# Part sums for the down product, emitted ahead of the S1 T1 product in each gate and up step

## The chip, the cores and the metric

The kernel runs on one core of a Trainium2 chip. The metric is the device time of one execution in microseconds; the times given are medians of several runs. The profile is one execution taken by the hardware profiler, with each engine's instructions, what they waited for, and the TensorE clock that was granted.

## The reference

An encoder trunk of two layers on a sequence of 1024 tokens of width 1024, in float32. Layer 0 has a chunked gMLP mixer, layer 1 a chunked attention with a relative bias; behind each stands a SwiGLU FFN, and the change lies in that FFN alone:

```python
def _swiglu_ffn(x, g_norm, w_gate_up, w_down):
    h = _rms_norm(x, g_norm)
    gate, up = jnp.split(h @ w_gate_up, 2, axis=-1)
    return (jax.nn.silu(gate) * up) @ w_down
```

The hidden width is 2816, 22 tiles of 128.

## The kernel before

Every matmul works on float32 numbers split into a high and a low part, so that a product of two 128 x 128 blocks takes three matmuls (high by high, high by low, low by high). The high part is made by a cast on ScalarE, the low part by a subtraction on VectorE (`split`, L116 to L118).

The gate and up product is done with a seven-product scheme for 2 x 2 blocks. One step `f` makes one tile of gate and one of up, for all 1024 tokens, with 7 products of 12 matmuls each: A11 B11, S2 T2, S1 T1, A12 B21, S3 T3, S4 B22 and A22 T4, in this order on TensorE. The A's and S's come from the step's two weight tiles (`quad_load`): A11 and A12 are the gate tile, S1 to S4 sums of gate and up made on GpSimd (L517, L518, L524, L525), A22 half of the up tile. The B's and T's come from the input, are made once, and stay in SBUF. There is one place for each kind of split weights, so the split of the next step's S12, A, S34 and A22 (`quad_s12`, `quad_a`, `quad_s34`, `quad_a22`) can begin when this step's products with them are through. The two raw tiles have one place each too: the next step's weights are loaded when this step's low parts are made.

The products of a step go into three PSUM banks, `pa`, `pb` and `pc`. `pb` takes S2 T2, S3 T3 and A22 T4 in turn: L793 and L804 read the sum out between them (`bu`), L833 reads the last (`yy`). `pc` takes S1 T1, is copied by ScalarE at L795 (`ac`), and then takes S4 B22, read at L823. `pa` takes A11 B11 (copied at L791) and A12 B21, which the gate reads (L701, and the SiLU at L702). `up` (L707, L708) makes y, the input of the down product.

For 16 of the 22 tiles of y the down product uses the same scheme, and needs sums and split parts of y. They are made during the gate and up loop by `y_parts`: when the odd step of a pair of tiles is done, five parts for that pair go into the list `todo`, and the steps that follow take them out with `some()`. They are `t12` (L683, L684: the sums for T1 and T2 in the tile `ty`), `t34` (L688, L691, a cast on ScalarE at L692, L693, and one transfer to DRAM at L694), and three times `out` (a cast at L676, the low part at L678, and two transfers, L679 and L680), for the second tile of the pair (`yo`), the first (`ye`) and `ty`. The first pair's parts are taken from f = 4 on, the last pair's at f = 18 and 19, in each of the two layers, 16 pairs in all.

In the kernel before, `some()` is called three times a step: behind the split of S12 (L797), behind the split of A (L802), and behind the split of S34 (L831). The step after a pair has even f and takes `t12`, `t34` and `out(1)`; the next has odd f and takes `out(0)` and `out(2)`.

The program's text isn't the order in which an engine works. A planner takes the instructions in the order in which they are emitted, works out what each waits for, and lays out one queue for each engine; on the chip each engine goes through its queue in order and waits for other engines by semaphores. SyncE's queue (SP) issues all transfers of this loop.

Of the kernel before, what the change touches and what calls it, by code (L numbers as in the profile page):

```python
# [49 lines left out]
class Trunk:  # L50
# [570 lines left out]
    def ffn(self, x, layer, sqp):  # L621
        nc, a = self.nc, self.a
        with ExitStack() as st:
# [16 lines left out]
            def bank():  # L640
                return psum.tile([P, 512], F32, name="ps")
# [19 lines left out]
            def outs(f):  # L661

                places = (0, 1, 4 if f == 1 else 6, (3, 5, 7)[f % 3])
                return [xplace(j, f"{n}{f}") for j, n in zip(places, ("ac", "bu", "gg", "yy"))]
# [3 lines left out]
            def y_parts(f):  # L668

                p = (f - 2) // 2  # L670
                ye, yo = ys.pop(f), ys.pop(f + 1)
                t = self.scratch(f"ty{f}")

                def out(n, y, place):
                    hi = xplace(place, f"yh{f}_{n}", F32R)
                    nc.scalar.copy(hi, y)  # L676
                    lo = y.bitcast(F32R)
                    TT(lo, y, hi.bitcast(F32), sub)  # L678
                    nc.sync.dma_start(td[p, 2 * n], hi.bitcast(F32))  # L679
                    nc.sync.dma_start(td[p, 2 * n + 1], y)  # L680

                def t12():
                    TT(t[:, t1], ye[:, t2], ye[:, t1], sub)  # L683
                    TT(t[:, t2], yo[:, t2], t[:, t1], sub)  # L684
                yield t12

                def t34():
                    TT(ye[:, t2], yo[:, t2], ye[:, t2], sub)  # L688
                    t4 = xplace(4, f"yt{f}", F32R)
                    r = t4[:, t2].bitcast(F32)  # L690
                    TT(r, yo[:, t1], t[:, t2], sub)  # L691
                    nc.scalar.copy(t4[:, t1], r)  # L692
                    TT(t4[:, t2], r, t4[:, t1].bitcast(F32), sub)  # L693
                    nc.sync.dma_start(td[p, 6], t4.bitcast(F32))  # L694
                yield t34
                yield lambda: out(1, yo, 2)
                yield lambda: out(0, ye, 4)
                yield lambda: out(2, t, 2)

            def gate(o, s, src):  # L700
                TT(o[2][:, HALF[s]], src, rbc[:, HALF[s]], mul)  # L701
                nc.scalar.activation(o[2][:, HALF[s]], o[2][:, HALF[s]], AF.Silu)  # L702

            def up(o, s, other, eng=None):

                y = o[3][:, HALF[s]]
                TT(y, y, rbc[:, HALF[s]], mul)  # L707
                TT(y, y, o[2][:, HALF[s]], mul)  # L708
# [28 lines left out]
            def prod(ps, A, b, start=False, stop=True):  # L737
                self.product(ps, q[A], (b, B), range(4), start, stop, True)
# [35 lines left out]
            def some(n=1):  # L774
                for _ in range(n):
                    if todo:
                        todo.pop(0)()

            for f in range(2, FT):
                more = f + 1 < FT  # L780
                if more:
                    qn = self.quad_load(layer, f + 1)
                    self.quad_places(qn, self.QUAD)
                else:
                    self.wlist, self.wnext = wl + (self.att_w if layer == 0 else []), 0
                o = outs(f)
                ac, bu, gg, yy = o
                pa, pb, pc = bank(), bank(), bank()

                prod(pa, "A11", "B11", True)  # L790
                nc.scalar.copy(ac[:, t1], pa)  # L791
                prod(pb, "S2", "T2", True)
                TT(bu[:, t1], pb, ac[:, t1], add)  # L793
                prod(pc, "S1", "T1", True)
                nc.scalar.copy(ac[:, t2], pc)  # L795
                self.quad_s12(qn) if more else self.prep_w()
                some()  # L797
                prod(pa, "A12", "B21")
                if f > 2:
                    gate(o, 0, pa)  # L800
                self.quad_a(qn) if more else self.prep_w()
                some()  # L802
                prod(pb, "S3", "T3")
                TT(bu[:, t2], pb, ac[:, t1], add)  # L804
                if f == 2:

                    bc = [bank(), bank()]
                    self.stats(None, bc[0], acc, rstd)
                    rbc = self.const.tile([P, S], F32, name="rbc")
                prod(pc, "S4", "B22", stop=True)  # L810
                if f == 2:
                    for s in range(2):
                        self.broadcast(self.hx, bc[s], rstd[:, 4 * s:4 * s + 4], rbc[:, HALF[s]], ("scr", 3))
                    for k in range(2):
                        _, _, g, y = late[k]
                        TT(g, g, rbc, mul)
                        nc.scalar.activation(g, g, AF.Silu)
                        TT(y, y, rbc, mul)
                        TT(y, y, g, mul)
                        nc.sync.dma_start(yd[k], y)  # L820
                    gate(o, 0, pa)
                TT(yy[:, t2], bu[:, t2], ac[:, t2], add)
                TT(gg[:, t2], pc, bu[:, t1], add)  # L823
                gate(o, 1, gg[:, t2])
                up(o, 1, None)
                if more:
                    self.quad_s34(qn)
                else:
                    d0 = self.down_load(layer, 0)
                    self.down_t1(d0)  # L830
                some()  # L831
                prod(pb, "A22", "T4", stop=True)
                TT(yy[:, t1], pb, ac[:, t1], add)  # L833
                up(o, 0, None)
                self.quad_a22(qn) if more else self.down_t2(d0)
                if f < FT - 4:
                    ys[f] = yy
                    if f % 2:
                        todo += y_parts(f - 1)
                else:  # L840
                    nc.sync.dma_start(yd[f], yy)
                q = qn
# [63 lines left out]
            for k in range(nq + 1):  # L906
# [22 lines left out]
                if k < nq:  # L929
# [7 lines left out]
                    else:  # L937
                        f = FT - 4 + k % 4
# [386 lines left out]
```

## Time and profile before

| | us |
|---|---|
| median of three runs | 2555.15 |
| lowest and highest run | 2554.9, 2555.91 |
| the profiled execution | 2560.03 |
| its span, first to last instruction | 2558.2 |

The mean granted TensorE clock of the profiled execution was 0.986 of full speed. In rows of instructions the columns are the start from the beginning of the span, the duration, engine, line, operation, the tile written and the tiles read, shape, and a count; in square brackets the idle time of the engine just before, and what ended it. PE is TensorE, DVE VectorE, ACT ScalarE, POOL GpSimd. Tile names drop their numbers: `wlo<-s,whi` is the low part of summed weights (S12 or S34), `wlo<-wraw,whi` that of loaded ones (A with 1024 columns, A22 with 512), `ty` the tile of T1 and T2, `yt` the tile of T4. Of the products' inputs `b1h`, `b1l`, `b2h` and `b2l` are the B's and T3, `bth` and `btl` T1 and T2, `bt` T4.

### The profile page before, as it was taken

The page shows a single profiled execution, that of the slowest core. Times are in us where ns is not written, and L with a number is a line of the kernel's source. Part 1 is how long each engine was busy: PE and PEld are TensorE (multiplying, and loading weights), DVE is VectorE, ACT ScalarE, POOL GpSimd, SP SyncE. Part 2 cuts the span into 40 slices and gives each one's busy share as a digit, 9 for nine tenths or more (in the row PEclk, how much of TensorE's full clock was granted, in tenths as well). Part 3 has the DMA queues.
Part 4 walks back from the last instruction along what each step waited for, and adds up shares of the span by engine and source line. Part 5 has one row for each costly group of instructions (what it writes and reads, how often), then busy time and mean ns, then how long its engine had stood idle before and what let it go on. Part 6 is the DMA issues. An engine that isn't in the chain of part 4 may idle for free.

```text
span 2558.2 us, 30686 instructions
## 1 busy us (share of the span) xinstructions
PE 2453.9 (96%) x11454; PEld 2018.4 (79%) x11454; DVE 1836.8 (72%) x2809; ACT 970.0 (38%) x1509; POOL 500.8 (20%) x413
## 2 busy tenths in 40 slices
PE   8999999999999999999999999989999999999997
PEld 7888888887777777788778887878877777777887
DVE  6227676688887876677777777778877778767775
ACT  5123232345433333212345555554453333332223
POOL 3001111121222222232211000000112222323411
PEclk9999999999999999999999999999999999999998
DMA  5232222232343434973312222252323434349731
GB/s 198 83 108 82 70 66 62 70 123 79 131 153 121 163 121 157 341 280 126 130 55 68 60 66 60 65 153 75 132 98 118 163 122 157 117 161 345 294 105 67
DMA packets 122390, 329.20 MB, mean 129 GB/s; under 512 B 11776, under 2 KB 44544, under 8 KB 122240
## 3 DMA queue, kind: packets, MB, share of 16 engines
q1 hardware_dynamic: 119936, 323.04, 37.1%
q10 hardware_dynamic: 2304, 4.20, 0.5%
q8 instruction: 90, 1.47, 0.2%
q14 instruction: 60, 0.49, 0.1%
HBM read 224.43 MB, written 94.37 MB: 125 GB/s over the span
## 4 chain that ended last, share of the span: by engine, by line
PE 65%; DVE 17%; DMA 6%; issue 5%; POOL 4%; ACT 3%; SPq 0%; DVEq 0%; POOLq 0%; ACTq 0%
PE ps L618 14%; PE ps L896 10%; PE pj L215 8%; PE ps L229 7%; PE ps L215 7%; DVE wlo L118 4%; DMA wraw<-wup 3%; PE pj L229 2%; PE po L1168 2%; PE ps L333 2%; PE ps L335 2%; PE ps L334 2%; PE pt L1141 2%; PE ps L456 1%; PE s L1118 1%
## 5 line engine op out<-in xcount | busy, mean ns | idle before, releaser
L117 ACT CAST whi<-wraw 128x1024 fp32r<-128x1024 f32 (+1 forms) x213 | 203.7, 961 | 365.2 <-PE ps L229 111.0
L118 DVE TENSOR_TENSOR wlo<-wraw,whi 128x1024 fp32r<-128x1024 f32 (+1 forms) x213 | 239.8, 1130 | 62.7 <-ACT whi L117 62.1
L896 PE MATMUL ps<-t,whi 128*128 128x512 f32 x896 | 278.1, 391 | 6.1 <-ACT whi L117 4.9
L517 POOL TENSOR_TENSOR s<-wraw 128x512 f32<-128x512 f32 x42 | 58.4, 1389 | 862.3 <-DMA wraw<-wup 521.0
L900 DVE TENSOR_TENSOR x<-x,ps 128x512 f32<-128x512 f32 x224 | 151.6, 684 | 74.3 <-PE ps L896 74.2
L896 PEld LDWEIGHTS ps<-t,whi 128*128 128x128 f32 x896 | 168.4, 189 | 43.4 <-ACT whi L117 5.7
L117 ACT CAST whi<-s 128x1024 fp32r<-128x1024 f32 x84 | 88.0, 1050 | 273.2 <-POOL s L518 242.6
L118 DVE TENSOR_TENSOR wlo<-s,whi 128x1024 fp32r<-128x1024 f32 x84 | 111.7, 1329 | 111.1 <-ACT whi L117 108.6
L896 PE MATMUL ps<-t,wlo 128*128 128x512 f32 x448 | 174.9, 390 | 0.0
L230 DVE TENSOR_TENSOR x<-x,ps 128x512 f32<-128x512 f32 (+1 forms) x176 | 113.2, 660 | 66.2 <-PE ps L229 62.4
L618 PE MATMUL ps<-bt,whi 128*128 128x512 f32 x336 | 116.8, 431 | 41.7 <-DVE bu L804 41.0
L618 PE MATMUL ps<-b2h,whi 128*128 128x512 f32 x368 | 147.1, 400 | 10.1 <-ACT ac L791 7.6
L215 PE MATMUL pj<-hhi,whi 128*128 128x512 f32 x368 | 151.1, 411 | 0.0
L215 PE MATMUL pj<-hlo,whi 128*128 128x512 f32 x368 | 148.1, 402 | 2.7 <-DVE hlo L118 2.7
L215 PE MATMUL pj<-hhi,wlo 128*128 128x512 f32 x368 | 146.7, 399 | 0.0
L618 PE MATMUL ps<-b1h,wlo 128*128 128x512 f32 x368 | 143.7, 390 | 2.7 <-DVE wlo L118 2.7
L396 POOL TENSOR_TENSOR mt<-mt,bbc 128x256 f32<-128x256 f32 x64 | 58.7, 918 | 445.5 <-ACT mt L395 442.5
L618 PE MATMUL ps<-b2h,wlo 128*128 128x512 f32 x368 | 145.4, 395 | 0.0
L618 PE MATMUL ps<-b2l,whi 128*128 128x512 f32 x368 | 145.4, 395 | 0.0
L618 PE MATMUL ps<-b1l,whi 128*128 128x512 f32 x368 | 143.5, 390 | 1.2 <-DVE b1l L118 1.2
L618 PE MATMUL ps<-b1h,whi 128*128 128x512 f32 x368 | 144.0, 391 | 0.1
L618 PE MATMUL ps<-bth,whi 128*128 128x512 f32 x336 | 130.7, 389 | 0.0
(367 smaller groups left out, 6490.3 us busy)
## 6 DMA issues: line engine op xcount, KB each, us to landing
t<-td SPq DMA_DIRECT2D x112, 512.0 KB, 7.8
td<-yh SPq DMA_DIRECT2D x48, 512.0 KB, 2.9
wraw<-wg SPq DMA_DIRECT2D x44, 512.0 KB, 3.6
wraw<-wup SPq DMA_DIRECT2D x44, 512.0 KB, 3.6
td<-yy SPq DMA_DIRECT2D x32, 512.0 KB, 2.7
wraw<-wds SPq DMA_DIRECT2D x32, 512.0 KB, 5.3
vd<-vt SPq DMA_DIRECT2D x32, 256.0 KB, 2.5
wraw<-wu SPq DMA_DIRECT2D x16, 512.0 KB, 3.7
```

What stands on the lines that cost most here:

```text
L117: self.nc.scalar.copy(hi, src)
L118: self.nc.vector.tensor_tensor(lo, src, hi.bitcast(F32), ALU.subtract)
L215: nc.tensor.matmul(ps[s], wt[:, c], ht[:, t], start=(kt == 0 and i == 0), stop=(kt == KT - 1 and i == 2),)
L229: nc.tensor.matmul(o, wt[:, c], yt[:, t], start=(j == 0 and i == 0), stop=(j == last and i == 2))
L230: nc.vector.tensor_tensor(x[d][:, t], x[d][:, t], o, ALU.add)
L333: nc.tensor.matmul(ps[tt], hhi[:, t], whi[:, c], start=(kt == 0), stop=False)
L334: nc.tensor.matmul(ps[tt], hhi[:, t], wlo[:, c], start=False, stop=False)
L396: nc.gpsimd.tensor_tensor(t2, t2, _bc_mid(bbc[:, g * P:(g + 1) * P], 2), ALU.add)
L517: nc.gpsimd.tensor_tensor(s12[:, HALF[0]], u[:, HALF[0]], u[:, HALF[1]], ALU.add)
L618: nc.tensor.matmul(ps, w[:, c], h, start=(start and i == pairs[0] and n == 0), stop=(stop and i == pairs[-1] and n == 2), skip_group_check ...
L896: nc.tensor.matmul(q[bank_], w[:, c], h, start=(start and i == 0 and n == 0), stop=(stop and i == 1 and n == 2), skip_group_check=True)
L900: TT(o, o, q[bank_], add)
```

## The change

In each step the three calls of `some()` are replaced by one, which stands behind the first add (L793) and ahead of the S1 T1 product. It takes three parts where f is even and two where f is odd. The parts themselves and their order in the list are the same.

```diff
                 TT(bu[:, t1], pb, ac[:, t1], add)
+                some(2 + (f + 1) % 2)
                 prod(pc, "S1", "T1", True)
                 nc.scalar.copy(ac[:, t2], pc)
                 self.quad_s12(qn) if more else self.prep_w()
-                some()
                 prod(pa, "A12", "B21")
                 if f > 2:
                     gate(o, 0, pa)
                 self.quad_a(qn) if more else self.prep_w()
-                some()
                 prod(pb, "S3", "T3")
...
                     self.down_t1(d0)
-                some()
                 prod(pb, "A22", "T4", stop=True)
```

## Rows read from the trace of the kernel before

**Rows 1.** The page's busy times: share of the span and instructions of each engine.

```profile
PE 2453.9 (96%) x11454; PEld 2018.4 (79%) x11454; DVE 1836.8 (72%) x2809; ACT 970.0 (38%) x1509; POOL 500.8 (20%) x413
```

**Rows 2.** Busy times by stretch: two pairs of steps, even then odd f.

```profile
core 0: us, PE busy (x) PEld busy (x) DVE busy (x) ACT busy (x) POOL busy (x), PEclk, DMA share, GB/s
911.40:932.80 21.40, 19.42 (x85) 15.70 (x85) 19.41 (x22) 8.88 (x12) 6.32 (x4) 1.00 0.43 150
932.80:952.50 19.70, 19.48 (x86) 15.62 (x85) 12.20 (x18) 6.13 (x9) 5.08 (x4) 1.00 0.37 131
702.40:725.20 22.80, 20.94 (x85) 16.84 (x85) 20.87 (x24) 8.86 (x12) 6.32 (x4) 0.93 0.49 168
725.20:744.30 19.10, 19.10 (x86) 15.80 (x85) 11.55 (x16) 6.61 (x10) 5.08 (x4) 1.00 0.28 104
```

**Rows 3.** Instructions in order of time, TensorE, an even step: S4 B22 and A22 T4.

```profile
925.05 0.39 PE L618 MATMUL ps<-b2h,whi 128*128 128x512 f32 x1
...
927.54 0.39 PE L618 MATMUL ps<-b2h,wlo 128*128 128x512 f32 x1
929.91 0.74 PE L618 MATMUL ps<-bt,whi 128*128 128x512 f32 x2 [1.98 <-DVE bu L804]
```

**Rows 4.** TensorE's groups: busy, mean ns, idle time ahead and what ended it.

```profile
L618 PE MATMUL ps<-b2h,whi 128*128 128x512 f32 x368 | 147.1, 400 | 10.1 <-ACT ac L791 7.6 <-ACT ac L747 1.2 <-ACT ac L795 1.1
...
L618 PE MATMUL ps<-bt,whi 128*128 128x512 f32 x336 | 116.8, 431 | 41.7 <-DVE bu L804 41.0 <-DVE bu L761 0.7
```

**Rows 5.** Instructions in order of time, VectorE, the same even step as rows 3.

```profile
914.69 0.68 DVE L683 TENSOR_TENSOR ty<-yy 128x512 f32<-128x512 f32 x1
917.16 0.69 DVE L793 TENSOR_TENSOR bu<-ps,ac 128x512 f32<-128x512 f32 x1 [1.78 <-PE ps L618]
...
918.93 1.77 DVE L688 TENSOR_TENSOR yy<-yy,yy 128x512 f32<-128x512 f32 x1
920.63 1.78 DVE L691 TENSOR_TENSOR yt<-yy,ty 128x512 f32<-128x512 f32 x1
922.52 2.13 DVE L678 TENSOR_TENSOR yy<-yy,yh 128x1024 fp32r<-128x1024 f32 x1
924.57 1.22 DVE L118 TENSOR_TENSOR wlo<-s,whi 128x1024 fp32r<-128x1024 f32 x1
925.70 0.68 DVE L693 TENSOR_TENSOR yt<-yt 128x512 fp32r<-128x512 f32 x1
...
926.91 1.21 DVE L678 TENSOR_TENSOR ty<-ty,yh 128x1024 fp32r<-128x1024 f32 x1
928.04 1.21 DVE L118 TENSOR_TENSOR wlo<-wraw,whi 128x1024 fp32r<-128x1024 f32 x1
929.17 0.68 DVE L804 TENSOR_TENSOR bu<-ps,ac 128x512 f32<-128x512 f32 x1
...
931.82 1.22 DVE L678 TENSOR_TENSOR yy<-yy,yh 128x1024 fp32r<-128x1024 f32 x1
932.96 0.69 DVE L701 TENSOR_TENSOR gg<-gg,rbc 128x512 f32<-128x512 f32 x1
```

**Rows 6.** Instructions in order of time, GpSimd: first and last sum of that step.

```profile
917.16 1.30 POOL L517 TENSOR_TENSOR s<-wraw 128x512 f32<-128x512 f32 x1 [12.85 <-DMA wraw<-wup]
...
921.94 1.62 POOL L525 TENSOR_TENSOR s<-wraw,s 128x512 f32<-128x512 f32 x1
```

**Rows 7.** Instructions in order of time, VectorE, the odd step that follows.

```profile
945.87 1.33 DVE L118 TENSOR_TENSOR wlo<-s,whi 128x1024 fp32r<-128x1024 f32 x1 [6.67 <-ACT whi L117]
```

**Rows 8.** Instructions in order of time, ScalarE, the even step of rows 3.

```profile
921.89 1.05 ACT L117 CAST whi<-s 128x1024 fp32r<-128x1024 f32 x1 [5.95 <-POOL s L518]
922.85 0.57 ACT L795 COPY ac<-ps 128x512 f32<-128x512 f32 x1
923.33 0.62 ACT L692 CAST yt<-yt 128x512 fp32r<-128x512 f32 x1
...
929.99 1.06 ACT L676 CAST yh<-yy 128x1024 fp32r<-128x1024 f32 x1 [2.34 <-DMA td<-yt]
```

**Rows 9.** Instructions in order of time, VectorE, first pair's even step in layer 0.

```profile
679.81 0.68 DVE L804 TENSOR_TENSOR bu<-ps,ac 128x512 f32<-128x512 f32 x1
680.41 1.21 DVE L678 TENSOR_TENSOR ty<-ty,yh 128x1024 fp32r<-128x1024 f32 x1
```

## The prediction

> **What bounds the kernel now.** I first read the busy shares of the page: TensorE is busy 96% of the span [rows 1], so a change can only win what TensorE waits for, or lose by making it wait more. The change touches only the gate and up loop (f = 2 to 21, twice), so the next view is the busy time by stretch, cut at the step boundaries [rows 2]. A step is 84 matmuls. Inside a product they follow each other at (927.54 - 925.05) / 11 = 0.226 us [rows 3], so a step without a wait takes 84 x 0.226 = 19.0 us. The two pairs of rows 2 take 41.1 and 41.9 us where 38.0 would do: 2.4 and 3.8 us too much in the step with even f, 0.7 and 0.1 in the step with odd f. With 16 pairs (f = 4 to 19, two layers) the whole loss is some 49 to 62 us, about 2% of the time, and that is the ceiling of any gain here.
>
> Where it goes is told by the groups of TensorE's instructions with the idle time ahead of each: the largest entry of this loop is A22 T4 waiting for the add at L804, 41.0 us in all [rows 4]. In the even step of rows 3, S4 B22 issues its last matmul at 927.54, and A22 T4 starts at 929.91, because it writes the bank that L804 reads, and L804 only ran from 929.17 to 929.85 [rows 5]. The step at 702.4 loses more than its wait, and its granted clock is 0.93 while the others have 1.00 [rows 2].
>
> Why L804 is late is read from VectorE's queue in the same step [rows 5]: from the first add (L793, 917.16) on there is no idle time. Ahead of L804 stand the second sum for T2 (between L793 and L688), L688, L691, the low part of yo (L678), the low part of the S12 weights (L118), that of T4 (L693), the gate multiply, the low part of ty (L678, 926.91), and the low part of the A weights. Three of the adds took 1.77, 1.78 and 2.13 us, where the same shapes take 0.68 and 1.21 us (L693 and the ty row), while GpSimd ran its weight sums from 917.16 to 923.56 [rows 5, 6]. In the odd step VectorE has 6.67 us of idle time in one piece [rows 7]. So the even step is VectorE's, the odd one is not.
>
> **What the order of emission decides.** This is the hinge. The rows show that the queues aren't in the order of emission; as I read them, the planner gives an engine the earliest emitted of what it holds to be ready. On ScalarE the cast of S12 (921.89) runs ahead of the copy L795 (922.85), though L795 is emitted first [rows 8]. On VectorE L683 (914.69) runs ahead of the add L793 (917.16), though it is emitted after it [rows 5]. And the low parts of ty (926.91) and ye (931.82) run in the even step, though they are emitted in the odd one [rows 5]. So emission is only a priority among ready things, and the change only matters where a part was ready and stood behind something that it is now emitted ahead of.
>
> **The change, part by part.** Nothing is added or removed: the same five parts a pair, with the same instructions and transfers, three in the even step and two in the odd one, as before (the third call of an odd step found an empty list). What moves:
>
> (1) The sums t12 (L683, L684), from behind the S12 split to behind L793. L683 already runs ahead of L793, and the rest right behind it [rows 5]. 0.
>
> (2) t34 (L688, L691, the cast L692, L693, and one transfer), from behind the A split. L688 and L691 already run right behind t12, with no weight work between them. L692 started at 923.33, as soon as the S12 cast (to 922.94) and the copy L795 (to 923.42) were through, while its input had been ready since 922.41, the end of L691 [rows 5, 8]. This is the one place where it stood behind something that it now precedes: L692 and L795 should swap on ScalarE. L692 gains 0.5 us, and L795 loses the 0.62 of L692. The S12 cast itself keeps its place unless the planner thinks L691 done before it; then it would have done so before, too, since nothing else was in ScalarE's way. L693 follows the low part of S12, which was being worked on anyway until 925.79; its price is 0, and the transfer of T4 goes out when it did. L795 would end at 923.42 + 0.62 = 924.04; S4 B22, which writes the bank that L795 reads, starts at 925.05 [rows 3]. So 0, with 1.0 us to spare; if the cover were gone, at most 0.62 us a pair. Its bounds are 0 and 16 x 0.62 = 9.9 us of loss; a gain on this edge is excluded, because no VectorE instruction leaves the stretch ahead of L804. I take 0, by the row that shows the 1.0 us.
>
> (3) The part out(1) (yo: a cast, L678, two transfers), from behind the S34 split. Its L678 is already the first long one behind L691 at 922.52, and ahead of the weights' low parts [rows 5]. 0.
>
> (4) out(0) and out(2), in the odd step, now behind the odd L793. They are still emitted after everything of the even step, and they already run there, at 926.91 and 931.82. Their rank against the even step's work is unchanged. 0.
>
> Transfers: SP's queue carries the parts' seven transfers between the loads of the next weights. These loads are emitted at the head of the step, ahead of the parts in both kernels, so no part passes a load. GpSimd gets no part, and its order of sums stays. No wait is added.
>
> The sum is 0 for each of the four. Against the profiled execution that is 2560.0 us again (a span of 2558.2 and 1.8 around it); this lies 4.9 us above the median of the three runs, 2555.15, to which I apply the 0. What a measurement of this kernel can tell from no change is about 0.2%, 5 us.
>
> A rule that speaks against the change: rows 5 and 6 show part sums of 0.68 us taking 1.78 while GpSimd works. The Trainium skill (SBUF — State Buffer, Who interferes with whom) says that a VectorE instruction with two SBUF inputs and a GpSimd instruction that reads SBUF lock each other out, the later one waiting in full. By that rule, work drawn forward into GpSimd's sums is work made dearer, and this kernel's rows agree.
>
> **The rivals.**
>
> F1, faster: the swap on ScalarE or a change of the planner's clock lets the low part of ty fall behind L804. In the first pair of layer 0 it does: L804 at 679.81, ty at 680.41 [rows 9]. Worth 928.04 - 926.91 = 1.13 us a pair, 16 x 1.13 = 18 us: 2537. For it: the order there differs from rows 5 by one rank only. Against: nothing on VectorE is moved by the change. 10%.
>
> F2, faster: the parts run where they are written, out(0) and out(2) in the idle time of the odd step. L804 of the even step comes 1.13 us sooner, and with 1.1 more from ye the last weight split too, which frees the odd step of its 0.7: 1.8 us a pair, 29 us, 2526. Against: the even step's VectorE takes whatever is ready [rows 5], and the change holds nothing back. 6%.
>
> S1, slower: the copy L795 behind the cast of T4 holds S4 B22. Price 0.62 us a pair, 9.9 us, 2565. It decides where L795 ends after S4 B22's turn. For it: TensorE waited for L795 1.1 us in all already [rows 4]. Against: 1.0 us to spare in rows 3 and 8, and a late S4 B22 is swallowed by the 2 us for which A22 T4 waits anyway. 10%.
>
> S2, slower: T4's transfer goes earlier, the place that it frees lets ye's cast (929.99, which waited for that transfer [rows 8]) go earlier, and its low part gets ahead of L804: 932.96 is the next start after 931.82, so about 1.14 us a pair, 18 us, 2573. It decides if that cast ends before 929.17 instead of 931.05. L693 can gain 1.13 us at most (by passing the low part of S12), so 1.9 us is out of reach of the rows; it can happen only in the planner's own idea of the times. 6%.
>
> S3, slower: the low parts of T4 and ty are drawn under GpSimd's sums and take 1.78 and 2.13 us for 0.68 and 1.21: 2.0 us a pair, 32 us, 2587. Against: the sums end at 923.56, and T4's cast, even swapped, ends at about 923.5 [rows 6, 8]. This is what the rule of the skill named above would do here. 2%.
>
> **How the numbers follow.** The forecast, the queue of VectorE unchanged, has 66%; that is also the rival "it doesn't do what it says" turned round: the text of the kernel changes and the order that runs does not. Time 2555.2, its own range 2550 to 2560. F1 and F2 make 16% for faster, S1, S2 and S3 18% for slower. The range takes in the forecast, F1 with its 2537 and S1 with its 2565, rounded up: 2537 to 2566. It leaves out F2, S2 and S3, 14%.
>
> **What would show it.** In the changed kernel's even steps, VectorE's instructions from L793 to L804 stand in the order of rows 5, L692 starts ahead of L795 on ScalarE, TensorE's wait for L804 stays at 41 us within some 5, and pairs take 41 to 42 us. It is wrong if ty or ye are found in odd steps or on the other side of L804 (F1, F2, S2), if TensorE's wait for L795 grows by more than a few us (S1), or if L693 or ty take twice their time (S3).

## The result and the profile after

| | us |
|---|---|
| before, median | 2555.1 |
| after, median (2507.32 to 2513.78) | 2508.05 |
| ratio after to before, 95% interval | 0.982 (0.9803 to 0.9837) |
| span of the profiled execution, before and after | 2558.2, 2512.0 |

The changed kernel is 47 us faster, just under the ceiling of 49 to 62 us that the prediction worked out from [rows 2]. The forecast was no change.

All steps from f = 4 to 19, one row a layer (in the columns of [rows 2]), in the kernel before:

```profile
662.00:998.10 336.10, 315.48 (x1346) 255.60 (x1345) 262.49 (x307) 123.22 (x161) 94.57 (x64) 0.98 0.41 144
1937.10:2274.80 337.70, 316.15 (x1346) 255.46 (x1346) 260.56 (x306) 122.94 (x161) 94.41 (x64) 0.98 0.41 143
```

And in the kernel after:

```profile
662.50:976.70 314.20, 307.27 (x1346) 251.63 (x1345) 242.05 (x306) 125.99 (x162) 96.47 (x64) 1.00 0.43 153
1913.30:2228.90 315.60, 307.43 (x1346) 251.65 (x1345) 243.09 (x308) 126.10 (x162) 95.88 (x64) 1.00 0.43 154
```

These 32 steps took 673.8 us and take 629.8: 44 of the 46 us between the spans. Unbroken they would take 32 x 19.0 = 608, so they lost 66 us and lose 22. Of the 44 us, 27 are time in which TensorE no longer waits; in the other 17 it does the same matmuls in less time, which is for the most part its clock, shown below.

The busy times by stretch of the kernel after: the pair of steps that [rows 2] show first, then the second pair, and the step with f = 19 of layer 0. Of the last, the kernel before is shown too, in the block of rows behind.

```profile
898.40:918.50 20.10, 19.33 (x85) 15.69 (x84) 16.98 (x22) 9.04 (x12) 7.02 (x4) 1.00 0.63 236
918.50:937.60 19.10, 19.10 (x86) 15.81 (x85) 13.04 (x19) 6.71 (x10) 5.09 (x4) 1.00 0.18 55
702.60:722.90 20.30, 19.38 (x86) 15.70 (x85) 18.80 (x22) 9.07 (x12) 7.01 (x4) 1.00 0.63 233
722.90:741.90 19.00, 19.00 (x85) 15.76 (x84) 12.93 (x19) 6.63 (x9) 5.10 (x4) 1.00 0.17 56
957.70:976.70 19.00, 19.00 (x86) 15.73 (x84) 12.23 (x18) 6.61 (x10) 5.08 (x4) 1.00 0.41 138
```

```profile
974.30:998.00 23.70, 20.91 (x85) 16.80 (x85) 13.33 (x18) 5.90 (x8) 5.09 (x4) 0.93 0.49 177
```

The two pairs took 41.1 and 41.9 us and take 39.2 and 39.3. Their odd steps are at the 19.0 us of 84 unbroken matmuls, the even ones lose 1.1 to 1.3 us, and f = 19 lost 4.7 us before and loses nothing now. In the even step VectorE's busy time fell from 19.41 to 16.98 us and in the odd one it rose from 12.20 to 13.04. TensorE's groups of A22 T4, before (in [rows 4]) and after:

```profile
L618 PE MATMUL ps<-bt,whi 128*128 128x512 f32 x336 | 107.4, 401 | 14.4 <-DVE bu L803 13.8 <-DVE bu L761 0.6
```

The wait for the second add (L804 before, L803 now) fell from 41.0 to 13.8 us. The busy time of these matmuls fell too, from 116.8 to 107.4 us. That is the clock: in eight of the 32 steps of the kernel before, f = 19 among them in both layers, the granted clock was 0.92 to 0.94, and in the kernel after it is 1.00 over all of them. In each of the eight the slow matmuls are those of A22 T4, right behind its wait for L804. In the step at 702.4 of [rows 2], for one, a matmul behind the wait takes 0.63 us where 0.39 is usual:

```profile
720.79 1.09 PE L618 MATMUL ps<-bt,whi 128*128 128x512 f32 x2 [1.86 <-DVE bu L804]
721.68 0.63 PE L618 MATMUL ps<-bt,wlo 128*128 128x512 f32 x1
```

So a part of these steps ran at the lower of the clock's two levels, 1.2 and not 2.4 GHz, after TensorE had stood idle (1.86 us in this row). TensorE's busy time in such a step was about 20.9 us where 19.4 was usual; eight times 1.5 us is some 12 us of the gain, by these rows.

VectorE's queue around the same even step, in order of time:

```profile
900.77 0.68 DVE L684 TENSOR_TENSOR ty<-yy,ty 128x512 f32<-128x512 f32 x1
...
901.98 0.68 DVE L688 TENSOR_TENSOR yy<-yy,yy 128x512 f32<-128x512 f32 x1
902.58 0.68 DVE L691 TENSOR_TENSOR yt<-yy,ty 128x512 f32<-128x512 f32 x1
903.36 1.23 DVE L678 TENSOR_TENSOR yy<-yy,yh 128x1024 fp32r<-128x1024 f32 x1
904.51 0.68 DVE L793 TENSOR_TENSOR bu<-ps,ac 128x512 f32<-128x512 f32 x1
905.11 1.19 DVE L693 TENSOR_TENSOR yt<-yt 128x512 fp32r<-128x512 f32 x1
906.97 1.56 DVE L678 TENSOR_TENSOR ty<-ty,yh 128x1024 fp32r<-128x1024 f32 x1 [0.68 <-ACT yh L676]
910.79 1.34 DVE L118 TENSOR_TENSOR wlo<-s,whi 128x1024 fp32r<-128x1024 f32 x1 [2.27 <-ACT whi L117]
...
913.79 1.21 DVE L678 TENSOR_TENSOR yy<-yy,yh 128x1024 fp32r<-128x1024 f32 x1
914.93 0.68 DVE L803 TENSOR_TENSOR bu<-ps,ac 128x512 f32<-128x512 f32 x1
...
922.56 0.69 DVE L683 TENSOR_TENSOR ty<-yy 128x512 f32<-128x512 f32 x1
```

The first parts aren't behind the first add, where the text of the kernel has them. The second sum for T2, L688, L691 and the low part of yo stand ahead of it, among VectorE's last work on the odd step's y, and fill the 1.78 us for which VectorE was idle there [rows 5]; and the next pair's first sum (L683) is made at 922.56, when only the even tile of that pair exists, where it used to wait for the end of the odd step ([rows 5], 914.69). Ahead of the first add the sums for T2 and T4 take 0.68 us each: they are through by 903.26, and GpSimd starts its weight sums at 903.96, as its instructions show:

```profile
903.96 1.79 POOL L517 TENSOR_TENSOR s<-wraw 128x512 f32<-128x512 f32 x1 [13.57 <-DMA wraw<-wup]
...
907.41 2.27 POOL L518 TENSOR_TENSOR s<-s,wraw 128x512 f32<-128x512 f32 x1
```

### The profile page after: what moved, and what is told of

It is laid out like the page before. It is cut to its first block, busy times and chain, and to the rows that moved or that the text cites. A ratio compares the mean times of both kernels' runs of the same rounds, so it can differ in the third digit from the quotient of the medians.

```text
span 2512.0 us, 30681 instructions
## 1 busy us (share of the span) xinstructions
PE 2437.1 (97%) x11454; PEld 2011.4 (80%) x11454; DVE 1799.3 (72%) x2809; ACT 975.4 (39%) x1509; POOL 502.9 (20%) x413
## 4 chain that ended last, share of the span: by engine, by line
PE 70%; DVE 13%; issue 5%; DMA 5%; POOL 4%; ACT 3%; POOLq 0%; DVEq 0%; ACTq 0%; SPq 0%
PE ps L618 17%; PE ps L894 11%; PE pj L215 8%; PE ps L229 8%; PE ps L215 7%; PE pj L229 3%; DVE wlo L118 3%; DMA wraw<-wup 3%; PE ps L333 2%; PE ps L334 2%; PE ps L335 2%; PE po L1166 2%; PE pt L1139 2%; POOL s L518 1%; POOL s L517 1%
## 5 line engine op out<-in xcount | busy, mean ns | idle before, releaser
L517 POOL TENSOR_TENSOR s<-wraw 128x512 f32<-128x512 f32 x42 | 64.6, 1538 | 818.4 <-DMA wraw<-wup 542.9
L618 PE MATMUL ps<-btl,whi 128*128 128x512 f32 x336 | 130.7, 389 | 0.0
```

The costliest lines, as they stand in the source:

```text
L517: nc.gpsimd.tensor_tensor(s12[:, HALF[0]], u[:, HALF[0]], u[:, HALF[1]], ALU.add)
L618: nc.tensor.matmul(ps, w[:, c], h, start=(start and i == pairs[0] and n == 0), stop=(stop and i == pairs[-1] and n == 2), skip_group_check ...
```

## The experiments

**Why the queues changed.** The kernel before had, in its trace, a row that the reading "the earliest emitted of what is ready" doesn't explain. In the odd step VectorE sat idle for 6.67 us up to 945.87 ([rows 7]), although the first sum of t12 needs only the even tile of y, complete at 937.79:

```profile
937.10 0.69 DVE L708 TENSOR_TENSOR yy<-yy,gg 128x512 f32<-128x512 f32 x1
...
956.51 0.69 DVE L683 TENSOR_TENSOR ty<-yy 128x512 f32<-128x512 f32 x1
```

So something else held L683. It writes `ty`, and `ty` is a tile of `scratch`, which has three places (`bufs=3` under the tag `scr`). The sums of S12 and S34 (`quad_s12`, `quad_s34`) take theirs from the same three. Theory P: a place goes to whoever writes its tile first in the order of emission, so the S12 sums, emitted ahead of t12 before the change and behind it after, took the place a step early and kept `ty` waiting. Theory R, the rival: what counts is the parts' rank on VectorE and ScalarE, and their grouping.

Four kernels tell the two apart. None of them adds a fourth place, which would test P from the other side.

One line moved in the kernel before:

```diff
+                some()
                 self.quad_s12(qn) if more else self.prep_w()
-                some()
```

> The kernel before, with one call of some() moved: the first of the three stands just ahead of the S12 split instead of just behind it; the other two stay. Theory P (place): the tile ty and the tiles of the S12 and S34 sums share three places; the sums of the next S12, emitted ahead of t12, take the place that ty needs, and ty gets one only when the S34 sums of the odd step are through. Then only the order of t12 and the S12 sums counts, and this kernel has the queues and the time of the changed kernel: 2508 us, within 5. Theory R (rank): the parts gain because all of them, three and two at a time, are ranked ahead of the step's other work on VectorE and ScalarE. Then moving one call past one split gives a third of the gain at most: 2540 us or more.

Measured: 2508.53 us, ratio 0.9832 (0.9813 to 0.985). One swapped pair of lines is the whole gain.

The changed kernel, its call moved down past the S12 split:

```diff
-                some(2 + (f + 1) % 2)
                 prod(pc, "S1", "T1", True)
                 nc.scalar.copy(ac[:, t2], pc)
                 self.quad_s12(qn) if more else self.prep_w()
+                some(2 + (f + 1) % 2)
```

> The changed kernel, with its one call of some(2 + (f + 1) % 2) moved down, from ahead of the S1 T1 product to just behind the S12 split. Theory P: the S12 sums are emitted ahead of t12 again and take the place, so the time is that of the kernel before: 2555 us, within 5, with the second sum for T2, L688 and L691 behind the first add. Theory R: the parts are still grouped and ranked ahead of the gate, of the A and of the S34 split, so most of the gain stays: 2510 to 2530 us.

Measured: 2553.64 us, ratio 1.0007 (0.9996 to 1.0019). Three and two at a time, behind the S12 split, is worth nothing. Its VectorE queue has the rows of the kernel before again, and its A22 T4 group the wait (in order of time; then by group):

```profile
915.16 0.69 DVE L793 TENSOR_TENSOR bu<-ps,ac 128x512 f32<-128x512 f32 x1 [0.99 <-PE ps L618]
915.76 0.68 DVE L684 TENSOR_TENSOR ty<-yy,ty 128x512 f32<-128x512 f32 x1
916.36 1.78 DVE L688 TENSOR_TENSOR yy<-yy,yy 128x512 f32<-128x512 f32 x1
```

```profile
L618 PE MATMUL ps<-bt,whi 128*128 128x512 f32 x336 | 115.6, 427 | 39.7 <-DVE bu L803 39.3 <-DVE bu L761 0.4
```

The kernel before, with nothing moved and one added instruction a pair that touches `ty` early:

```diff
                 t = self.scratch(f"ty{f}")
+                claims.append(t)
...
+                if claims and f % 2 == 0:
+                    nc.vector.memset(claims.pop()[:, 0:1], 0.0)
                 self.quad_s12(qn) if more else self.prep_w()
                 some()
```

> The kernel before with nothing moved; in each even step one VectorE instruction that sets one column of ty to zero is emitted ahead of the S12 split (16 in all, t12 overwrites the column). It only makes ty take its place earlier. Theory P: the queues of the changed kernel and 2508 to 2514 us. Theory R: no part has another rank, so 2555 us, or up to 3 more for the added instructions.

Measured: 2511.71 us, ratio 0.9848 (0.9827 to 0.9869). No part changed its rank, and the gain is there. In the odd step the added write runs at once, and the first sum (L684 in this kernel) right behind it, in what was the idle time of [rows 7]:

```profile
920.98 0.06 DVE L799 MEMSET ty<- 128x1 f32 x1
921.09 0.69 DVE L684 TENSOR_TENSOR ty<-yy 128x512 f32<-128x512 f32 x1
```

The changed kernel, with the writers of the S12 tile alone put ahead of the parts:

```diff
+                if more:
+                    self.quad_sum12(qn, self.scratch("s12"))
                 some(2 + (f + 1) % 2)
                 prod(pc, "S1", "T1", True)
```

> The changed kernel, in which only the two GpSimd sums of S12 are emitted ahead of the parts; the parts stay ahead of the S1 T1 product and of all splits. Theory P: the S12 sums take the place first, and the time is that of the kernel before: 2555 us, within 6. Theory R: the parts' rank on VectorE and ScalarE is that of the changed kernel, so 2508 us, within 5.

Measured: 2555.55 us, ratio 1.0014 (1.0003 to 1.0025). All parts rank as in the changed kernel, and the gain is gone. On its VectorE L688 takes the slow 1.78 us again:

```profile
915.52 1.78 DVE L688 TENSOR_TENSOR yy<-yy,yy 128x512 f32<-128x512 f32 x1
```

The four agree with P and none with R. That the tiles' places are what is fought for follows from the claim in both directions. Which tile's release ended the wait of `ty` in the kernel before was not taken apart: behind its idle time VectorE works without a break from 945.87 until L683 runs at 956.51, so the place may have come free anywhere in between.

**What the gain is made of.** The nearest of the prediction's rivals, F2, had stood at 29 us. The next kernels ask what the gain consists of. First the changed kernel again, on the chip of the three that follow.

> The changed kernel once more, on the same chip as the three that follow. Both theories below: 2508 us, within 5.

Measured: 2512.07 us, ratio 0.983 (0.9814 to 0.9846).

Then GpSimd is kept from all but a few reads (8 columns of each tile), in both kernels alike; S34 is treated as S12:

```diff
-        nc.gpsimd.tensor_tensor(s12[:, HALF[0]], u[:, HALF[0]], u[:, HALF[1]], ALU.add)
-        nc.gpsimd.tensor_tensor(s12[:, HALF[1]], s12[:, HALF[0]], g[:, HALF[0]], ALU.subtract)
+        nc.gpsimd.tensor_tensor(s12[:, 0:8], u[:, 0:8], g[:, 0:8], ALU.add)
+        nc.gpsimd.memset(s12[:, 8:512], 0.02)
+        nc.gpsimd.memset(s12[:, 512:1024], 0.02)
```

> The kernel before, with its queues on VectorE as they are; GpSimd sums only 8 columns of each half of the S12 and S34 tiles and fills the rest with a constant, which reads nothing from SBUF. It leaves out the weight sums. This asks what the gain of the change is made of. Theory C (collision): the part sums behind the first add are slow because GpSimd reads at the same time: L688, L691 and the low part of yo fall from 1.77, 1.78 and 2.13 us to 0.68, 0.68 and 1.21, 3.1 us a pair, more than the 2 us for which A22 T4 waits, so that the wait for L804 nearly goes: 2500 to 2515 us with all parts still in the even step. Theory N (number): the even step has simply too many VectorE instructions ahead of L804, whatever each takes; then the wait stays for the most part and the time is 2535 us or more.

Measured: 2476.42 us, ratio 0.9694 (0.9679 to 0.9708). This is 24 us below the lower end of what C expected, and N is out. The steps of f = 4 to 19 lose nothing here (layer 0; layer 1 takes 304.60 us too):

```profile
652.60:957.20 304.60, 304.60 (x1345) 252.22 (x1344) 233.07 (x307) 123.17 (x162) 35.88 (x96) 1.00 0.45 158
```

That is 64.6 of the 85 us between this trace's span and that of the kernel before. C had counted the wait for L804 alone; the odd steps, f = 19 and the clock come on top. The other 20 us lie outside these steps and weren't taken apart. VectorE has the queue of the kernel before, parts behind the first add and all five in the even step, and the slow ones are at 0.68, 0.69 and 1.23 us (lines are two higher than in rows 5):

```profile
886.76 0.69 DVE L795 TENSOR_TENSOR bu<-ps,ac 128x512 f32<-128x512 f32 x1 [1.94 <-PE ps L620]
887.36 0.68 DVE L686 TENSOR_TENSOR ty<-yy,ty 128x512 f32<-128x512 f32 x1
887.96 0.69 DVE L690 TENSOR_TENSOR yy<-yy,yy 128x512 f32<-128x512 f32 x1
888.57 0.69 DVE L693 TENSOR_TENSOR yt<-yy,ty 128x512 f32<-128x512 f32 x1
889.36 1.23 DVE L680 TENSOR_TENSOR yy<-yy,yh 128x1024 fp32r<-128x1024 f32 x1
...
895.11 0.68 DVE L806 TENSOR_TENSOR bu<-ps,ac 128x512 f32<-128x512 f32 x1
```

The second add starts 895.11 - 886.76 = 8.4 us behind the first, where it took 929.17 - 917.16 = 12.0 in [rows 5]; 3.1 of the 3.7 us between them are the three shorter instructions, and 0.57 is the second sum for T2, which the prediction's three slow rows left out. In the kernel before it was:

```profile
917.76 1.25 DVE L684 TENSOR_TENSOR ty<-yy,ty 128x512 f32<-128x512 f32 x1
```

VectorE has no idle time between the two adds in either trace, so in this step the shorter instructions, and not the earlier S12, bring the second add forward. A22 T4 waits for it nowhere in the loop (by group):

```profile
L620 PE MATMUL ps<-bt,whi 128*128 128x512 f32 x336 | 103.8, 390 | 0.5 <-DVE bu L763 0.5
```

> The changed kernel with the same replacement on GpSimd; it leaves out the weight sums. Theory C: what is left to gain by a free GpSimd is the collision of L693 (1.19 for 0.68 us) and the low part of ty (1.56 for 1.21) and the wait for S12, which make most of the 0.8 us that A22 T4 still waits in an even step: 2490 to 2500 us, 10 to 20 below the changed kernel. Theory N: as C, since few instructions stand ahead of L804 here; the two differ in the run before.

Measured: 2470.82 us, ratio 0.9674 (0.9658 to 0.969), well below the 2490 to 2500 expected. Between the two orders of the parts there are 2553.2 - 2512.1 = 41 us with GpSimd's reads and 2476.4 - 2470.8 = 6 us without; in the traces the 32 steps take 609.2 and 609.7 us, so what is left of the difference isn't in them. The change pays only beside GpSimd's reads. This replacement also makes S12 earlier, and over the whole loop the collision isn't separated from the late S12 by it; the rows above give the collision's 3.6 us in one even step.

**What was left in the changed kernel.** In its even step the low part of ye (913.79) stands just ahead of the second add (914.93), and A22 T4 still waits, as TensorE's row shows:

```profile
915.66 0.73 PE L618 MATMUL ps<-bt,whi 128*128 128x512 f32 x2 [0.77 <-DVE bu L803]
```

The edit takes that part behind the second add and holds it there:

```diff
+                yield lambda: out(2, t, 2)
                 yield lambda: out(0, ye, 4)
-                yield lambda: out(2, t, 2)
...
-                some(2 + (f + 1) % 2)
+                if f % 2 == 0:
+                    some(4)
...
-                TT(bu[:, t2], pb, ac[:, t1], add)
+                bu2 = TT(bu[:, t2], pb, ac[:, t1], add)
+                if f % 2 == 0:
+                    with self.tc.issue_after(bu2.ins):
+                        some()
```

> The changed kernel, with the order of the last two parts exchanged, four parts taken behind the first add of the even step, and the fifth, that of ye, taken in the same step right behind the second add (L804 of before), with its instructions held behind that add on each engine that both use (VectorE). In the changed kernel the low part of ye stands just ahead of that add and takes 1.14 us of the 0.8 us by which A22 T4 waits. If that is what is left of the wait, the even steps lose none of their 1.0 us: 14 x 1.0 = 14 us less than the changed kernel, 2494 us, within 4. If the wait is for S12, which VectorE got late, it stays, and the time is 2508 us, within 4.

Measured: 2501.49 us, ratio 0.979 (0.9775 to 0.9804), 10.6 us below the changed kernel on the same chip: the wait was that part for the most, but the gain isn't the 14 us expected. The group of A22 T4 waits 3.2 us where it waited 13.8:

```profile
L618 PE MATMUL ps<-bt,whi 128*128 128x512 f32 x336 | 105.7, 396 | 4.4 <-DVE bu L804 3.2 <-DVE bu L761 1.0
```

Since the collision is a cost, the sums can also go where they can't collide. On this kernel, first repeated:

> The kernel of e8_out0_late once more, beside the two that follow: 2501 us, within 5.

Measured: 2499.86 us, ratio 0.9783 (0.9758 to 0.9807). All four weight sums by VectorE (`nc.vector` for `nc.gpsimd` in L517, L518, L524 and L525):

> The kernel of e8_out0_late with all four weight sums of a step on VectorE in place of GpSimd: 4 instructions of 0.68 us (starts 0.60 apart) more on VectorE in each step, and nothing on GpSimd to collide with. If the collision and the late S12 are the larger cost, each even step loses nothing any more and f = 3, which waited 3.8 us, loses less: 2485 to 2495 us. If VectorE's number of instructions is, the 2.4 us a step more put the second add behind its turn again: 2515 us or more.

Measured: 2483.08 us, ratio 0.972 (0.9698 to 0.9742). VectorE has four instructions a step more, and A22 T4's wait for the second add of a step is gone:

```profile
L618 PE MATMUL ps<-bt,whi 128*128 128x512 f32 x336 | 103.7, 390 | 1.1 <-DVE bu L761 1.1
```

With the S12 sums alone on VectorE:

> The kernel of e8_out0_late with the two S12 sums on VectorE and the two S34 sums on GpSimd. Half of the added work and, of the collisions, those with S34's sums left. If the late S12 is what an even step waits for: 2488 to 2497 us. If the collisions with what GpSimd still does cost as much as the moved sums save: 2501 us, within 4.

Measured: 2486.73 us, ratio 0.9733 (0.9706 to 0.976). 13 of the 17 us come with S12; whether by its earlier end or by half as many collisions isn't separated here. Last, the kernel before with its four sums on VectorE and every part where it was:

> The kernel before, with all four weight sums of a step on VectorE and nothing else changed: parts emitted where they were, the fifth not held back. If the order of the parts mattered above all because it laid them under GpSimd's reads, it matters little here: ahead of the second add stand about 12 VectorE instructions at starts 0.6 or 1.14 us apart, some 8 us, in time for A22 T4 (10.7 us behind the first add), so 2480 to 2495 us, within 12 of e10_late_sums_on_vector. If the even step's number of parts costs by itself, it has four instructions more than before and the time is 2510 us or more.

Measured: 2483.7 us, ratio 0.9721 (0.9703 to 0.9738). The order of the parts, which the change and e8 together made worth 54 us (2553.9 to 2499.9), is worth nothing that can be told once GpSimd doesn't read (2483.1 against 2483.7, ratios of 0.972 and 0.9721, each against the kernel before on its own chip). The steps of f = 4 to 19 lose nothing in this kernel's trace (layer 0; layer 1 takes 304.60 us too):

```profile
658.30:962.90 304.60, 304.60 (x1345) 252.23 (x1344) 268.74 (x371) 124.09 (x161) 0.00 (x0) 1.00 0.45 159
```

This kernel and e10 are the fastest here of those that leave nothing out, some 25 us below the changed kernel.

## Why the prediction was wrong

**The bound was nearly right.** The wait for L804 as the place of the loss, VectorE's even step as its cause and the sums under GpSimd as slow rows all held. The ceiling of 49 to 62 us was a little low: it took two pairs for all, and the 32 steps lost 66 us, f = 19 alone 4.7 in each layer. The change won 44 of them; e12 wins nearly all.

**The step that failed is the hinge**, "the planner gives an engine the earliest emitted of what it holds to be ready ... So emission is only a priority among ready things". It left out that emission also decides who gets a place for a tile when several tiles share places. Step (1), t12 at 0, follows from it and is the very step that carried the gain: t12's rank on VectorE indeed didn't matter (e3), but its first write now comes ahead of the S12 sums' first write. The trace had the contradiction in rows that the prediction used: 6.67 us of idle time in [rows 7] with L683's input ready since 937.79. The prediction read this idle time as room, and didn't ask why a ready part of lowest rank wasn't in it.

**Steps (2) to (4)** fail with it. The swap of L692 and L795 on ScalarE didn't come as told: the cast L692 runs at 903.29 now, ahead of even the S12 cast, since L691 itself went ahead of the first add, as ScalarE's rows show:

```profile
903.29 0.62 ACT L692 CAST yt<-yt 128x512 fp32r<-128x512 f32 x1 [0.15 <-DVE yt L691]
...
906.84 0.58 ACT L796 COPY ac<-ps 128x512 f32<-128x512 f32 x1
909.71 1.05 ACT L117 CAST whi<-s 128x1024 fp32r<-128x1024 f32 x1 [2.29 <-POOL s L518]
```

In (3) the low part of yo moved ahead of the first add. In (4) the parts of ye and ty stayed in the even step, as forecast, but earlier in it, while the first sum of t12, which (1) had left in its place, moved into the odd step.

**The statement on transfers**, that no part passes a load, fails too. In the even step of f = 18 the low part of ty (`td<-ty`) and the high part of ye (`td<-yh`) stood behind the load of the next gate weights, and they go ahead of it now. SP's rows before, and then after:

```profile
970.91 0.33 SPq L496 DMA_DIRECT2D wraw<-wg  x1
971.29 0.42 SPq L680 DMA_DIRECT2D td<-ty  x1
...
975.07 3.01 SPq L859 DMA_DIRECT2D x<-xd  x2
979.39 0.32 SPq L841 DMA_DIRECT2D yd<-yy  x1
979.76 0.42 SPq L496 DMA_DIRECT2D wraw<-wup  x1
```

```profile
951.84 0.32 SPq L679 DMA_DIRECT2D td<-yh  x1
953.08 0.33 SPq L496 DMA_DIRECT2D wraw<-wg  x1
...
954.59 1.46 SPq L857 DMA_DIRECT2D x<-xd  x2
959.77 0.33 SPq L496 DMA_DIRECT2D wraw<-wup  x1
```

That by itself cost nothing: in both kernels the load goes out within 0.1 us of the end of the low part of A (970.83 and 953.01), which frees its place. The up weights for the step behind f = 19 went out 5.5 us into f = 19, and now go out 2.1 us into it. Of these 3.4 us, 2.4 are VectorE's: the low part of A22, which frees their place, ended at 978.76, 4.5 us into the step, and now ends at 959.74, 2.0 us into it. For the other 1.0 us they stood behind two loads for the down product (L859) and a transfer of y. They landed 5.4 us after their issue, and now 3.6. All this goes with the 4.7 us of f = 19 that are gone; no experiment took this part alone.

**The rivals.** F2 was the right direction at 6%, with the wrong mechanism: out(0) and out(2) don't wait for the odd step that they are written in. What moves is the front of the five parts, ahead of the even step's first add, and the first sum of t12 alone goes into the odd step before it. Its 1.8 us a pair measured 1.9 and 2.6 in the two pairs shown, and some 1.5 of the 2.6 are the clock of the step at 702.4. The pairs of f = 18 and 19 gain 6.4 us in each layer (in layer 0 45.5 us before, from 952.5 to 998.0, and 39.1 after, from 937.6 to 976.7), 13 us in all. The other 14 pairs gain 44 - 13 = 31 us, near F2's 29 for 16; that is luck, since six of these pairs had a step at the lower clock, some 9 us that F2 hadn't priced. What F2's sum lacked is the clock, the step f = 19, and the end of the collision (1.09, 1.10 and 0.90 us for L688, L691 and yo), part of which comes back in L693 and ty.

S3's mechanism did happen: L693 took 1.19 and ty 1.56 us in the changed kernel, under GpSimd's sums. The Trainium skill's rule (SBUF — State Buffer, Who interferes with whom) agrees with these rows. And e6 and e12 show the sums on GpSimd, by collision and by the late S12, as the largest cost of the loop. S3 failed because it priced what comes under the sums and not what goes out from under them. S2's place, ye ahead of the second add, is where the changed kernel stands (913.79 and 914.93), and e8 measured it at about 11 us. S1's swap has no place in the new queue.

## What to carry to other kernels

Where a planner lays out the queues, moving a line can matter by what it claims first, not by what it runs first: before a move is priced, list which tiles share places with the tile that the moved code writes, and who writes theirs on the way. An engine that is idle while a ready instruction of low rank isn't run is a sign of such a claim; one added early write of a column tests it. And where two engines slow each other, look at what the move takes out of their common time before counting instructions.

## What wasn't expected of the hardware

VectorE and GpSimd in each other's way cost the loop more than its number of VectorE instructions. Moving the four weight sums of each step from GpSimd (1.3 us each alone, up to 2.27 in collision) to VectorE (0.68 us each) adds 2.7 us of VectorE work a step to an engine that was the loop's bound in every second step, and the kernel gets 68 us faster (e12, 2552.1 to 2483.7): nothing collides, and S12 doesn't wait for GpSimd. In layer 0's steps of f = 4 to 19 VectorE's busy time rose from 262.5 to 268.7 us, and TensorE lost nothing any more.

A wait also cost more than its own length: in eight of the 32 steps TensorE's clock fell to the lower level behind a wait of A22 T4, which made such a step some 1.5 us longer again.
